# A two-layer encoder trunk on one NeuronCore: the activations' tiles begin 32 bytes later in SBUF, on multiples of 64 bytes, and the weights' tiles keep their place within 64 bytes

## The chip, the cores and the metric

The kernel runs on one core of a Trainium2 chip. The metric is the device time of one execution in microseconds (us); less is better. Before the change it was 1282.45 us, the median of 3 runs (1281.79 to 1290.47). One further execution was recorded by the hardware profiler; it took 1282.87 us.

## The reference, cut to what matters

The input is `x` of 256 positions by 1024 features, all in float32. Two layers of one block follow each other:

```python
for l in range(DEPTH):                                    # 2
    x = x + 0.5 * swiglu(rmsnorm(x, ffn1_norm[l]), ffn1_w_gate[l], ffn1_w_up[l], ffn1_w_down[l])
    proj = rmsnorm(x, mix_norm[l]) @ w_in[l]              # q, k, v, lru x, lru gate, memory q, 3 gates
    ...
    br_attn = window_attention(q, k, v, attn_sinks[l]) @ w_attn_out[l]
    br_lru = rglru_branch(xr, yr, ...) @ w_lru_out[l]
    br_mem = memory_attention(cq, rmsnorm(mem, mem_norm[l]), w_mem_kv[l]) @ w_mem_out[l]
    merged = g[:, :, 0] * br_attn + g[:, :, 1] * br_lru + g[:, :, 2] * br_mem
    x = x + merged @ w_out[l]
    x = x + 0.5 * swiglu(rmsnorm(x, ffn2_norm[l]), ffn2_w_gate[l], ffn2_w_up[l], ffn2_w_down[l])
return rmsnorm(x, final_norm)
```

The feed-forward width is 2816. The weights are some 226 MB in float32, read once, and nearly all of the arithmetic is their products with 256 columns of activations.

## The kernel before, in words

**The weights.** They are packed on the host as 432 slabs of 8 blocks; a block is 128 by 128. `load` (L176 to L180) brings a slab of 512 KB from HBM into one of 5 `st` tiles. `prep` splits it in two parts of type float32r, which TensorE takes in one pass: ScalarE rounds it into `whi` (L194), and VectorE writes the rest, `st - whi`, into `wlo` (L195). There are 5 tiles of each. Loads run up to 5 slabs ahead and splits up to 3 slabs ahead of the block in use.

**The products.** `gemm` goes over the blocks of one 128-row strip of outputs. The activations are split likewise and lie in `Halves` tiles: for each k, 256 columns of the high part and then 256 of the low part. Each block is one matmul of 512 columns (both halves under `whi`, L219) and one of 256 (the high half under `wlo`, L220):

```python
mm(both, hi, X.both(k), start=(k == 0), stop=False)                  # L219
mm(out[:, 0, :], lo, X.hi(k), start=False, stop=(k == n - 1))        # L220
```

The second argument is the stationary operand, which a weight load (`LDWEIGHTS`, PEld in the profile) brings into the array; the third is the moving operand, streamed past it column by column. There are 3,316 such blocks. A few places differ. `mem_kv` makes the values of the memory (tile `mv`, L622 to L624) the other way round: slices of the activations are stationary, and 512 columns of `whi` or `wlo` move. `singles` (L236 to L238, the last 2 strips of the kernel) and the LRU gates take three matmuls of 256 columns to a block. The attention scores and values (`ws`, `ms`, L946) are plain float32, which the array takes in two passes, each of which is a record in the trace.

**The order.** Each engine's instructions stand in the order in which the code is recorded; between the blocks a list of delayed tasks (`at`, `tick`) places the rest of the work, one tick to a slab.

**SBUF.** `pools` opens one pool after another, and each lies behind the one before in every partition. A tile takes a multiple of 32 bytes. The constants come first, then `big` (14 tiles of 8,192 bytes: `x`, all `Halves`, the projections), `h4`, `s2`, `s1`, `sm`, then `stage` (the `st` tiles), and last `hl` (`whi`, `wlo`). The four tiles of the constants take 1,056 + 2,560 + 1,024 + 640 = 5,280 bytes, which is 82 times 64 and 32 more. As they begin on a multiple of 64, every pool behind begins 32 bytes past one, and as nearly all later tiles are multiples of 64 bytes long, so do their tiles: `x` at byte 21,792 of its partition, the first `st` at 166,688, the first `whi` at 187,168. The small `sm` tiles (8 or 16 bytes in 32) alternate.

Of the kernel before, what the change touches and what calls it, by code (L numbers as in the profile page):

```python
# [19 lines left out]
F32 = mybir.dt.float32  # L20
# [74 lines left out]
class Trunk:  # L95
# [17 lines left out]
    def pools(self, ctx):  # L113
        tc = self.tc
        e = ctx.enter_context
        self.pc = e(tc.tile_pool(name="const", bufs=1))
        self.pbig = e(tc.tile_pool(name="big", bufs=14))
        self.ph4 = e(tc.tile_pool(name="h4", bufs=3))
        self.ps2 = e(tc.tile_pool(name="s2", bufs=4))
        self.ps1 = e(tc.tile_pool(name="s1", bufs=3))  # L120
        self.psm = e(tc.tile_pool(name="sm", bufs=2))
        self.pst = e(tc.tile_pool(name="stage", bufs=5))
        self.phl = e(tc.tile_pool(name="hl", bufs=5))
        self.pmm = e(tc.tile_pool(name="mm", bufs=3, space=bass.MemoryType.PSUM))
        self.patt = e(tc.tile_pool(name="att", bufs=2, space=bass.MemoryType.PSUM))
# [931 lines left out]
```

## Time and profile before

| | us | share of the span |
|---|---|---|
| median of 3 runs | 1282.45 | |
| the profiled execution | 1282.87 | |
| its span, first to last instruction | 1281.1 | |
| TensorE matmul (PE) busy | 1265.4 | 99% |
| TensorE weight load (PEld) busy | 1104.4 | 86% |
| VectorE (DVE) busy | 985.7 | 77% |
| ScalarE (ACT) busy | 761.3 | 59% |
| the 16 DMA engines, weights' queue | | 57% |

How to read it: matmuls are pipelined. [...] What a matmul costs the next one is the distance between their starts. PEclk is the granted share of TensorE's clock; at 1.00 it is the upper of the two levels, 2.4 GHz, at which 512 columns at one a cycle are 213.3 ns and 256 are 106.7 ns.

### The profile page before, as it was taken

What the parts mean: (1) busy time and instruction counts of PE and PEld (TensorE: products, weight loads), DVE (VectorE), ACT (ScalarE), POOL (GpSimd) and SP (SyncE); (2) the same over time, 40 slices, a digit from 0 to 9 for tenths busy, and PEclk for the clock granted to TensorE, in tenths of its full rate; (3) what the DMA queues carried; (4) which work ended last, traced back from release to release, by engine and by line L of the source; (5) the groups of instructions that cost most, each with busy time, mean ns of one, the idle gap of its engine ahead of it and who ended that gap; (6) DMA issues with size and microseconds to landing.
All of it is one profiled execution on the core that took longest, in us unless ns stands there. A gap on an engine that the chain in (4) does not pass through costs nothing.

```text
span 1281.1 us, 19099 instructions
## 1 busy us (share of the span) xinstructions
PE 1265.4 (99%) x7318; PEld 1104.4 (86%) x7318; DVE 985.7 (77%) x1406; ACT 761.3 (59%) x1134; POOL 0.3 (0%) x5
## 2 busy tenths in 40 slices
PE   8999999999999999999999999999999999999997
PEld 7888888888888888888888888888888888888886
DVE  7788766888789987677678775669887898876754
ACT  5656544588577565555456564447867675655542
POOL 0000000000000000000000000000000000000000
PEclk9999999999999999999999999999999999999998
DMA  8665665555445566666656665564554465665651
GB/s 288 209 189 167 214 183 179 172 175 166 144 131 187 187 197 189 195 187 202 194 184 208 189 188 195 167 204 156 183 165 132 148 199 180 197 195 185 195 184 48
DMA packets 64748, 232.40 MB, mean 181 GB/s; under 512 B 7313, under 2 KB 7441, under 8 KB 64401
## 3 DMA queue, kind: packets, MB, share of 16 engines
q1 hardware_dynamic: 64224, 230.65, 57.2%
q8 instruction: 58, 0.95, 0.3%
q10 hardware_dynamic: 432, 0.53, 0.1%
q14 instruction: 34, 0.27, 0.1%
HBM read 230.10 MB, written 1.05 MB: 180 GB/s over the span
## 4 chain that ended last, share of the span: by engine, by line
PE 90%; DVE 5%; ACT 3%; issue 1%; DMA 1%; SPq 0%; DVEq 0%; ACTq 0%
PE pd L219 12%; PE pg L219 11%; PE pu L219 11%; PE pd L220 6%; PE pgt L219 6%; PE pu L220 6%; PE pg L220 6%; PE pbr L219 5%; PE pgt L220 3%; DVE wlo L195 2%; PE pyr L219 2%; PE pwo L219 2%; PE pbr L220 2%; PE pxr L219 2%; PE pgu L219 2%; PE pcq L219 1%
## 5 line engine op out<-in xcount | busy, mean ns | idle before, releaser
L195 DVE TENSOR_TENSOR wlo<-st,whi 128x1024 fp32r<-128x1024 f32 (+2 forms) x438 | 524.6, 1206 | 238.1 <-ACT whi L194 238.0
L194 ACT ACTIVATE whi<-st 128x1024 fp32r<-128x1024 f32 (+2 forms) x438 | 443.5, 1045 | 39.5 <-PE pd L219 20.5
L219 PE MATMUL pd<-h,whi 128*128 128x512 f32 x660 | 230.1, 393 | 0.0
L219 PE MATMUL pg<-xs,whi 128*128 128x512 f32 x640 | 225.2, 394 | 0.0
L219 PE MATMUL pu<-xs,whi 128*128 128x512 f32 x640 | 225.1, 393 | 0.0
L220 PE MATMUL pd<-h,wlo 128*128 128x256 f32 x660 | 184.9, 280 | 0.0
L220 PE MATMUL pg<-xs,wlo 128*128 128x256 f32 x640 | 179.3, 280 | 0.8 <-DVE wlo L195 0.8
L220 PE MATMUL pu<-xs,wlo 128*128 128x256 f32 x640 | 179.3, 280 | 0.0
L219 PEld LDWEIGHTS pd<-h,whi 128*128 128x128 f32 x660 | 123.6, 187 | 28.1
L219 PEld LDWEIGHTS pg<-xs,whi 128*128 128x128 f32 x640 | 119.9, 187 | 27.0
L219 PEld LDWEIGHTS pu<-xs,whi 128*128 128x128 f32 x640 | 119.8, 187 | 26.9
L219 PE MATMUL pgt<-xs,whi 128*128 128x512 f32 x384 | 139.2, 405 | 0.0
L220 PEld LDWEIGHTS pd<-h,wlo 128*128 128x128 f32 x660 | 124.7, 189 | 0.0
L220 PEld LDWEIGHTS pg<-xs,wlo 128*128 128x128 f32 x640 | 120.9, 189 | 1.1 <-DVE wlo L195 1.1
L220 PEld LDWEIGHTS pu<-xs,wlo 128*128 128x128 f32 x640 | 121.0, 189 | 0.0
L220 PE MATMUL pgt<-xs,wlo 128*128 128x256 f32 x384 | 107.6, 280 | 0.0
L219 PEld LDWEIGHTS pgt<-xs,whi 128*128 128x128 f32 x384 | 72.1, 188 | 19.5 <-issue 3.0
L258 ACT COPY g<-pg 128x512 f32<-128x512 f32 x40 | 23.5, 586 | 99.7 <-PE pg L220 92.9
L220 PEld LDWEIGHTS pgt<-xs,wlo 128*128 128x128 f32 x384 | 72.5, 189 | 0.2
L270 ACT ACTIVATE h<-u 128x512 fp32r<-128x512 f32 x44 | 27.8, 632 | 46.2 <-DVE u L523 43.9
L320 ACT ACTIVATE xs<-x,pk 128x256 fp32r<-128x256 f32 x40 | 18.7, 503 | 49.2 <-DVE x L559 21.6
L219 PE MATMUL pgu<-xs,whi 128*128 128x512 f32 x128 | 44.7, 394 | 1.2 <-DVE xs L324 1.2
(237 smaller groups left out, 2053.5 us busy)
## 6 DMA issues: line engine op xcount, KB each, us to landing
st<-wpack SPq DMA_DIRECT2D x428, 512.0 KB, 3.8
st<-wpack SPq DMA_DIRECT2D x8, 256.0 KB, 4.9
mem<-memT SPq DMA_DIRECT2D x2, 1024.0 KB, 6.7
x<-xT SPq DMA_DIRECT2D x4, 256.0 KB, 5.0
outT<-xg SPq DMA_DIRECT2D x2, 256.0 KB, 2.6
outT<-xg ACTq DMA_DIRECT2D x2, 256.0 KB, 2.7
cst<-cst SPq DMA_DIRECT2D x1, 320.0 KB, 7.8
pk<-pk SPq DMA_DIRECT2D x1, 128.0 KB, 7.5
```

Source lines behind the costliest of these rows:

```text
L194: nc.scalar.activation(hi[:, c], st[:, c], AF.Copy)
L195: nc.vector.tensor_tensor(lo[:, c], st[:, c], hi[:, c].bitcast(F32), op=ALU.subtract)
L219: mm(both, hi, X.both(k), start=(k == 0), stop=False)
L220: mm(out[:, 0, :], lo, X.hi(k), start=False, stop=(k == n - 1))
L258: self.nc.scalar.copy(dst, ps[:, :, 1, :])
L270: hi = lambda: self.nc.scalar.activation(X.hi(k, n), src, AF.Copy)
L320: self.t.nc.scalar.activation(self.xs.hi(k), x[:, k, :], AF.Copy, scale=self.t.vec(self.v, self.l, k))
```

## The change

Two pools of one tile each are opened that nothing ever uses, each 32 bytes (8 float32) of every partition. `gapx` lies behind the constants and moves all pools behind it by 32 bytes; `gap` lies ahead of `hl` and moves this pool by 32 more.

```diff
         self.pc = e(tc.tile_pool(name="const", bufs=1))
+        e(tc.tile_pool(name="gapx", bufs=1)).tile([128, 8], F32, name="gapx")
         self.pbig = e(tc.tile_pool(name="big", bufs=14))
         self.ph4 = e(tc.tile_pool(name="h4", bufs=3))
         self.ps2 = e(tc.tile_pool(name="s2", bufs=4))
         self.ps1 = e(tc.tile_pool(name="s1", bufs=3))
         self.psm = e(tc.tile_pool(name="sm", bufs=2))
         self.pst = e(tc.tile_pool(name="stage", bufs=5))
+        e(tc.tile_pool(name="gap", bufs=1)).tile([128, 8], F32, name="gap")
         self.phl = e(tc.tile_pool(name="hl", bufs=5))
```

Where the tiles begin, in bytes of a partition, and what is left of that over a multiple of 64:

| tiles | before | over 64 | after | over 64 |
|---|---|---|---|---|
| constants (`pk`, `cst`, `Rm`, `lc`) | 16,512 to 21,152 | 0 or 32 | the same | the same |
| `big` (first: `x`) | 21,792 | 32 | 21,824 | 0 |
| `h4`, `s2`, `s1` (first: `P`) | 136,480 | 32 | 136,512 | 0 |
| `st` | 166,688 | 32 | 166,720 | 0 |
| `whi` | 187,168 | 32 | 187,232 | 32 |
| `wlo` | 207,648 | 32 | 207,712 | 32 |

In the built program every instruction, its place on its engine and its semaphores are the same as before; only addresses differ.

## Rows read from the trace of the kernel before

**Rows 1.** The page: span, busy time by engine, and TensorE's clock in 40 slices.
```profile
span 1281.1 us, 19099 instructions
PE 1265.4 (99%) x7318; PEld 1104.4 (86%) x7318; DVE 985.7 (77%) x1406; ACT 761.3 (59%) x1134; POOL 0.3 (0%) x5
PEclk9999999999999999999999999999999999999998
```
**Rows 2.** The chain of work that ended last, by engine.
```profile
PE 90%; DVE 5%; ACT 3%; issue 1%; DMA 1%; SPq 0%; DVEq 0%; ACTq 0%
```
**Rows 3.** Groups by line, whole span: xcount | busy us, mean ns | idle before.
```profile
L219 PE MATMUL pd<-h,whi 128*128 128x512 f32 x660 | 230.1, 393 | 0.0
L219 PE MATMUL pg<-xs,whi 128*128 128x512 f32 x640 | 225.2, 394 | 0.0
...
L220 PE MATMUL pg<-xs,wlo 128*128 128x256 f32 x640 | 179.3, 280 | 0.8 <-DVE wlo L195 0.8
```
**Rows 4.** TensorE's matmuls in order of time from 500 us: start us, us.
```profile
499.79 0.39 PE L219 MATMUL pu<-xs,whi 128*128 128x512 f32 x1
500.02 0.28 PE L220 MATMUL pu<-xs,wlo 128*128 128x256 f32 x1
...
532.72 0.39 PE L219 MATMUL pu<-xs,whi 128*128 128x512 f32 x1
```
**Rows 5.** The same from 130 us.
```profile
129.62 0.40 PE L219 MATMUL pu<-xs,whi 128*128 128x512 f32 x1
129.86 0.28 PE L220 MATMUL pu<-xs,wlo 128*128 128x256 f32 x1
...
162.84 0.40 PE L219 MATMUL pd<-h,whi 128*128 128x512 f32 x1
```
**Rows 6.** Groups by line, TensorE, 500 to 620 us and then 100 to 200 us.
```profile
L219 PE MATMUL pd<-h,whi 128*128 128x512 f32 x114 | 39.6, 391 | 0.0
L219 PE MATMUL pd<-h,whi 128*128 128x512 f32 x176 | 62.2, 399 | 0.0
```
**Rows 7.** Matmuls in order of time: 512 columns after 512, from 211 us.
```profile
211.30 0.39 PE L622 MATMUL mv<-whi,xs 128*128 128x512 f32 x1
...
214.02 0.39 PE L622 MATMUL mv<-whi,xs 128*128 128x512 f32 x1
```
**Rows 8.** Groups by line, TensorE, 212 to 215, 17.9 to 18.8, 66.0 to 66.5 us.
```profile
L622 PE MATMUL mv<-whi,xs 128*128 128x512 f32 x4 | 1.6, 389 | 0.0
L219 PE MATMUL pg<-xs,whi 128*128 128x512 f32 x1 | 0.4, 389 | 0.0
L220 PE MATMUL pu<-xs,wlo 128*128 128x256 f32 x1 | 0.3, 276 | 0.0
```
**Rows 9.** Weight loads in order of time, 17 to 19 us and at 279.5 us.
```profile
17.67 0.19 PEld L219 LDWEIGHTS pg<-xs,whi 128*128 128x128 f32 x1
18.93 0.19 PEld L220 LDWEIGHTS pg<-xs,wlo 128*128 128x128 f32 x1 [1.07 <-DVE wlo L195]
...
279.53 0.19 PEld L219 LDWEIGHTS pyr<-xs,whi 128*128 128x128 f32 x1
279.63 0.19 PEld L220 LDWEIGHTS pyr<-xs,wlo 128*128 128x128 f32 x1
```
**Rows 10.** The longest pieces of the chain: plain float32 matmuls, start us, us.
```profile
330.08 1.73 PE ms L913 x8
367.72 3.45 PE mv L946 x16
```
**Rows 11.** Matmuls in order of time: 256 columns after 256, 1256 us.
```profile
1256.01 0.28 PE L236 MATMUL pd<-h,whi 128*128 128x256 f32 x1
1256.12 0.28 PE L237 MATMUL pd<-h,whi 128*128 128x256 f32 x1
1256.24 0.28 PE L238 MATMUL pd<-h,wlo 128*128 128x256 f32 x1
1256.37 0.28 PE L236 MATMUL pd<-h,whi 128*128 128x256 f32 x1
```
**Rows 12.** Groups by line and shape: VectorE and ScalarE at 1024 and 512 columns.
```profile
L195 DVE TENSOR_TENSOR wlo<-st,whi 128x1024 fp32r<-128x1024 f32 x428 | 519.2, 1221 | 238.1 <-ACT whi L194 238.0
L508 DVE TENSOR_TENSOR g<-g,R 128x512 f32<-128x512 f32 x44 | 30.4, 692 | 1.5
L194 ACT ACTIVATE whi<-st 128x1024 fp32r<-128x1024 f32 x428 | 438.3, 1056 | 38.9 <-PE pd L219 20.5 <-issue 10.5 <-PE mv L624 4.7
L509 ACT ACTIVATE g<-g 128x512 f32<-128x512 f32 x44 | 27.7, 633 | 27.4 <-DVE g L508 27.1
```
**Rows 13.** Stretches: length, busy us (count) by engine, clock, DMA share, GB/s.
```profile
0.00:30.00 30.00, 25.82 (x143) 22.33 (x144) 22.98 (x51) 19.15 (x30) 0.30 (x5) 1.00 0.86 296
400.00:455.00 55.00, 55.00 (x319) 48.11 (x318) 50.43 (x68) 34.44 (x52) 0.00 (x0) 1.00 0.62 195
455.00:640.00 185.00, 185.00 (x1072) 163.07 (x1071) 133.09 (x172) 101.49 (x130) 0.00 (x0) 1.00 0.62 192
```

## The prediction

> **What bounds the kernel now.** The first view is the page's list of engines [rows 1]: TensorE's matmuls cover 1265.4 of the 1281.1 us, at a granted clock that is full nearly throughout, so at 2.4 GHz. The chain that ended last gives TensorE 90% [rows 2]. VectorE at 77% and ScalarE at 59% keep ahead of it; a group of 640 matmuls waits 0.8 us in all [rows 3]. So the end moves only if TensorE's own pace moves, and the pace has to be read from the distances between starts.
>
> From 499.79 to 532.72 us lie 95 blocks (a matmul of 512 and one of 256 columns each), which is 346.6 ns per block [rows 4]. From 129.62 to 162.84 us lie 94, which is 353.4 ns [rows 5]. At one column a cycle 768 columns would take 320.0 ns. So there are a quick and a slow pace, and both are 27 to 33 ns above the columns' own time. The mean duration of the 512-column matmul tells the pace of a stretch: 391 ns in a quick one, 399 in a slow one [rows 6]. Over the whole span it is 393 and 394 [rows 3], so between a quarter and three eighths of the feed-forward blocks run at the slow pace. With a third, a block takes 348.9 ns, and the 3,316 blocks take 1,157 us.
>
> **Where the loss of a block comes from.** The value product of the memory runs 512 columns after 512: 12 matmuls from 211.30 to 214.02 us, 226.7 ns each, at 389 ns duration [rows 7, 8]. So a record is 162 ns longer than its stream. One matmul of 512 columns ran with no weight load beside it: the next load comes at 18.93 us, 1.15 us after its start (17.78 us), held up by `wlo` [rows 9]. It took 389 ns too [rows 8], a stream of about 227 ns. A lone one of 256 columns took 276 ns, a stream of about 114 [rows 8]. Against 213.3 and 106.7 ns the two lose 13.4 and about 7 ns. The loss without a weight load is thus in proportion to the columns, and close to one cycle of 0.417 ns in 16 columns (32 x 0.417 = 13.3; 16 x 0.417 = 6.7). 16 columns of float32r are 64 bytes of a partition.
>
> The plain float32 matmuls read the same kind of tile, also 32 bytes past a multiple of 64, but take two cycles for each column: 8 records of 256 columns in 1.73 us and 16 in 3.45 us, 216 ns each [rows 10], against 213.3 for 512 cycles. They lose 2.7 ns per record, not 13. So it is the supply of the moving operand that runs short at one float32 a cycle, once in 64 bytes, and at half that rate it keeps up. VectorE and ScalarE show nothing like it: from 512 to 1024 columns VectorE needs 1221 - 692 = 529 ns more and ScalarE 1056 - 633 = 423 [rows 12], steady steps of 1.03 and 0.83 ns, slower than TensorE's 0.417.
>
> **The change part by part.** *The two gaps* add no instruction, no transfer and no wait; the built programs differ in addresses alone. Their direct cost is 0. *The `st` tiles* move too, which touches the DMAs that write them and the first operand of each split; both run ahead of TensorE, and a gain there stays hidden. *The weights' tiles* keep their place within 64 bytes, so a weight load by itself keeps its time: two in a row start 0.10 us apart at 279.53 us [rows 9]. *The moving operand of nearly all matmuls* now begins on a multiple of 64. Before, each run of 16 columns counted from the operand's start lay across two 64-byte lines; now it lies in one. No matmul in this trace has a start of the other kind at one float32 a cycle, so the price is bounded from both sides.
>
> Bound of no gain: the cycle is lost at each crossing of a line, and 512 columns make 32 of them (now 31): 0 us. Bound of full gain: the loss goes, and what the two-cycle matmuls lose stays, 2.7 ns [rows 10]. Then 512 columns take 216.0 ns and 256 take 109.4, a block 325.4, and the sum is 3,316 x (348.9 - 325.4) = 78 us. Between them: the 256-column matmul may be held by the load of the next weights rather than by its stream. Three such matmuls in a row start at 1256.01, 1256.12, 1256.24 and 1256.37 us, 120 ns each [rows 11], more than the stream of 114, and a block at the quick pace leaves 346.6 - 230 = 117 ns for it [rows 4]. With 216.0 + 116.7 = 332.7 a block gains 16.2 ns, the sum 54 us. If also the slow pace with its 6.8 ns stayed everywhere, 339.5 remain and 31 us are gained. I take 54 us, since the rows of 256 after 256 say that this matmul waits for more than its columns. The value product and `singles` gain nothing: in the one the weights move, and the other stands at 120.
>
> *What takes some of it back.* In the first 30 us TensorE waits for data at 296 GB/s (25.82 of 30 us busy) [rows 13]; some 60 blocks gain nothing, 1 us. VectorE is busiest between 400 and 455 us, 50.43 of 55 [rows 13]; at a pace 4.6% quicker this is 96%, so it still fits. The weights come at 192 GB/s in a steady stretch [rows 13] and would come at 201, below the 296 of the start. So 53 us remain: 1282.9 - 53 = 1230. The profiled execution stands 0.4 us above the median, which I neglect.
>
> [...]
>
> **The rivals.**
> *Nothing changes (1282 us).* The cycle in 64 bytes may belong to the crossing itself, or to float32r at full rate, wherever the operand begins. For it: every start in the trace is alike, so nothing in it shows a dependence, and the distances are regular to a nanosecond over 33 us. Against it: nothing, but a read path that falls short by one cycle in 17 for every operand would be odd. The slow and quick paces may be dealt out anew, as they follow interruptions: all quick is 3,316 x 2.3 = 8 us less (1275), all slow 3,316 x 4.5 = 15 us more (1297).
> *A smaller gain.* Only the slow pace goes, or only the 512-column stream gains a part: 1251 to 1268 us. I count this with the first case as "faster".
> *Slower.* Moving and stationary operand began at the same place within 64 bytes, and now begin half a line apart. The weight load beside a 512-column matmul is free at best now (389 ns with and without [rows 8]). If the two reads come to meet, every block pays for it. The place is each block; the price is bounded by the slow pace everywhere, 1297 us, and by the longest distances within it, about 0.24 us for a 512-column matmul and 0.12 for a 256 (129.62 to 129.86 us is the former [rows 5]), 360 ns a block, 37 us, 1320. It decides as soon as the loss per block exceeds 4 ns. [...]
>
> **How the numbers follow.** I give the gain (1204 to 1268 us, likeliest 1230) 0.43, no change (1275 to 1297) 0.37, the loss (1297 to 1320) 0.20. The likeliest is the gain, and its own range is 1204 to 1252. Both signs hold much of the chance, so the range of 8 in 10 reaches from 1208 (some 0.04 lie below) to 1301 (some 0.16 above). About 1%, 13 us, is what a measurement of this kernel can tell from no change. Faster by more than that: 0.43; within: 0.37; slower: 0.20.
>
> **What would show it.** If the step is right, a quick stretch shows blocks of 325 to 333 ns, the 512-column matmul at about 378 ns instead of 391, the value product unchanged at 389 (its moving operand stays 32 past a line), and the plain float32 matmuls unchanged at 216. If the rival of no change holds, 391 and 346.6 stand as they were. If the reads meet, the 512-column matmul grows above 399 ns and the 256-column one with it, and the value product, whose two operands now differ as well, grows too. My forecast is wrong if the lost cycle stays with operands that begin on a line, or if the 256-column matmul takes up what the 512 gives.

## The result, and the profile after

The changed kernel takes **1293.18 us** (1291.48 to 1294.36), against 1282.6 for the kernel before in the same rounds: a ratio of 1.008, 95% interval 1.0063 to 1.0096. Forecast were 1230. The time moved by less than 1%, and to the other side.

The page of the changed kernel, its span, engines and clock, answers to [rows 1]:

```profile
span 1290.9 us, 19099 instructions
PE 1276.4 (99%) x7318; PEld 1107.9 (86%) x7318; DVE 985.9 (76%) x1406; ACT 762.5 (59%) x1134; POOL 0.3 (0%) x5
PEclk9999999999999999999999999999999999999998
```

TensorE alone has grown, its matmuls by 11.0 us of busy time at the same count of instructions and the same clock; VectorE and ScalarE stand where they were. The page's groups by line (two lines of code are added, so L221 is L219 of before, and L222 is L220) answer to [rows 3]:

```profile
L221 PE MATMUL pd<-h,whi 128*128 128x512 f32 x660 | 233.4, 397 | 0.0
L221 PE MATMUL pg<-xs,whi 128*128 128x512 f32 x640 | 227.8, 397 | 0.0
L222 PE MATMUL pg<-xs,wlo 128*128 128x256 f32 x640 | 180.0, 281 | 0.0
```

The 512-column matmul did not fall from 391 to the 378 ns of a right forecast. Its mean went from 393 and 394 to 397, to the side of the slow pace. The matmuls in order of time from 500 us, the stretch of [rows 4] (start us, us):

```profile
499.94 0.40 PE L221 MATMUL pu<-xs,whi 128*128 128x512 f32 x1
500.18 0.28 PE L222 MATMUL pu<-xs,wlo 128*128 128x256 f32 x1
500.30 0.39 PE L221 MATMUL pu<-xs,whi 128*128 128x512 f32 x1
500.53 0.28 PE L222 MATMUL pu<-xs,wlo 128*128 128x256 f32 x1
500.64 0.40 PE L221 MATMUL pu<-xs,whi 128*128 128x512 f32 x1
...
532.80 0.39 PE L221 MATMUL pu<-xs,whi 128*128 128x512 f32 x1
```

From 499.94 to 532.80 us lie 93 blocks, 353.3 ns each, where the kernel before ran at 346.6 [rows 4]. So no new pace came, but the slow one where the quick one was. In detail it is another slow pace: here two blocks repeat (0.36 and 0.35 us), while the slow stretch of before [rows 5] repeats after three. Over the two traces, with a block called quick where the mean distance of the seven around it is under 350 ns (distances over 390 ns, which hold a wait, left out), the kernel before has 2,144 quick ones of 3,263 in a row and the changed one 548; the mean of either kind is nearly the same in both, 346.7 and 353.3. (2,144 - 548) x 6.6 ns = 10.5 us, which is the whole difference of the medians (10.6).

The stretches answer to [rows 13] (length, busy us and count by engine, clock, DMA share, GB/s): in the same 185 us TensorE starts 1,053 matmuls where it started 1,072.

```profile
400.00:455.00 55.00, 55.00 (x314) 47.75 (x313) 49.89 (x67) 33.45 (x51) 0.00 (x0) 1.00 0.59 193
455.00:640.00 185.00, 185.00 (x1053) 160.85 (x1052) 131.28 (x170) 101.12 (x130) 0.00 (x0) 1.00 0.60 186
```

And the value product, 512 columns after 512, in order of time [rows 7]:

```profile
211.18 0.39 PE L626 MATMUL mv<-whi,xs 128*128 128x512 f32 x1
211.41 0.40 PE L624 MATMUL mv<-whi,xs 128*128 128x512 f32 x1
...
213.28 0.39 PE L626 MATMUL mv<-whi,xs 128*128 128x512 f32 x1
```

Nine distances in 2.10 us are 233.3 ns, against 226.7 before. This is the sign that the prediction named for two reads that meet, though its moving operand (the weights) keeps its place within 64 bytes.

**The theories.** A: the step of the prediction, an operand that begins on a multiple of 64 loses no cycle (fallen with the result, unless the weights' own place hid the gain). B: the pace hangs on the place of the weights against that of the activations, modulo 64 bytes. C: the same, but modulo a longer period (the change moves the weights from a distance of 0 to one of 32 modulo 512). D: only the instant at which a stretch begins deals out the pace. I first thought of B; C came out of the bursts and the padded tiles below.

### The profile page after: what moved, and what is told of

Read it like the earlier page. It is cut to its first block, busy times and chain, and to the rows that moved or that the text cites. A ratio compares the mean times of both kernels' runs of the same rounds, so it can differ in the third digit from the quotient of the medians.

```text
span 1290.9 us, 19099 instructions
## 1 busy us (share of the span) xinstructions
PE 1276.4 (99%) x7318; PEld 1107.9 (86%) x7318; DVE 985.9 (76%) x1406; ACT 762.5 (59%) x1134; POOL 0.3 (0%) x5
## 4 chain that ended last, share of the span: by engine, by line
PE 92%; DVE 4%; ACT 2%; issue 1%; DMA 1%; SPq 0%; DVEq 0%; ACTq 0%
PE pd L221 12%; PE pg L221 11%; PE pu L221 11%; PE pgt L221 7%; PE pd L222 6%; PE pu L222 6%; PE pg L222 6%; PE pbr L221 5%; PE pgt L222 3%; PE pyr L221 2%; PE pbr L222 2%; PE pwo L221 2%; DVE wlo L197 2%; PE pxr L221 2%; PE pgu L221 2%; PE pwo L222 1%
## 5 line engine op out<-in xcount | busy, mean ns | idle before, releaser
L221 PE MATMUL pd<-h,whi 128*128 128x512 f32 x660 | 233.4, 397 | 0.0
L221 PE MATMUL pu<-xs,whi 128*128 128x512 f32 x640 | 228.0, 397 | 0.0
L221 PE MATMUL pg<-xs,whi 128*128 128x512 f32 x640 | 227.8, 397 | 0.0
L222 PE MATMUL pd<-h,wlo 128*128 128x256 f32 x660 | 185.8, 282 | 0.0
L222 PE MATMUL pu<-xs,wlo 128*128 128x256 f32 x640 | 180.0, 281 | 0.0
L222 PE MATMUL pg<-xs,wlo 128*128 128x256 f32 x640 | 180.0, 281 | 0.0
L221 PEld LDWEIGHTS pd<-h,whi 128*128 128x128 f32 x660 | 123.9, 188 | 30.7
L221 PEld LDWEIGHTS pu<-xs,whi 128*128 128x128 f32 x640 | 120.2, 188 | 29.2
L221 PEld LDWEIGHTS pg<-xs,whi 128*128 128x128 f32 x640 | 120.1, 188 | 29.1
L221 PE MATMUL pgt<-xs,whi 128*128 128x512 f32 x384 | 139.0, 403 | 0.0
L222 PEld LDWEIGHTS pd<-h,wlo 128*128 128x128 f32 x660 | 124.4, 188 | 0.0
L222 PEld LDWEIGHTS pu<-xs,wlo 128*128 128x128 f32 x640 | 120.6, 189 | 0.0
L222 PEld LDWEIGHTS pg<-xs,wlo 128*128 128x128 f32 x640 | 120.6, 188 | 0.0
L222 PE MATMUL pgt<-xs,wlo 128*128 128x256 f32 x384 | 107.9, 281 | 0.0
L221 PEld LDWEIGHTS pgt<-xs,whi 128*128 128x128 f32 x384 | 72.1, 188 | 19.3 <-issue 2.3
L222 PEld LDWEIGHTS pgt<-xs,wlo 128*128 128x128 f32 x384 | 72.4, 189 | 0.2
L221 PE MATMUL pgu<-xs,whi 128*128 128x512 f32 x128 | 45.3, 396 | 1.0 <-ACT whi L196 1.0
```

## The experiments

### The places within 64 bytes, one by one

`act0_w0` opens `gapx` alone, so that activations and weights both begin on multiples of 64. `act32_w0` opens `gap` alone: the activations stay, and the weights move by 32. `all_64on` moves everything by 64 bytes, which keeps every residue modulo 64.

```diff
# act0_w0                                  # all_64on: [128, 16]
+ e(tc.tile_pool(name="gapx", bufs=1)).tile([128, 8], F32, name="gapx")
# act32_w0, ahead of hl
+ e(tc.tile_pool(name="gap", bufs=1)).tile([128, 8], F32, name="gap")
```

> Only gapx, so every tile behind the constants begins on a multiple of 64: moving and stationary operand lie alike again, as in the kernel before. Theory of the distance (the pace is worse where the two operands begin half of 64 bytes apart): blocks in layer 1's feed-forward parts at 346.6 ns, time 1275 to 1286 us. Theory of the moving operand (its start on a multiple of 64 is what costs): 353.5 ns per block and 1291 to 1295 us, as after the change. Theory of the deal (no address matters; each waiting point deals the quick or the slow pace anew): anywhere from 1275 to 1297 us.

> Only gap, so the activations stay 32 bytes past a multiple of 64 and the weights' tiles begin on one: half of 64 bytes apart, the other way round than after the change. Theory of the distance: 353.5 ns per block nearly throughout, 1291 to 1295 us. Theory of the moving operand: as before, 1281 to 1286 us, quick blocks of 346.6 ns in layer 1. Theory of the deal: anywhere from 1275 to 1297 us.

> gapx of 64 bytes alone: all tiles behind the constants move by 64, so nothing changes modulo 64 against the kernel before. Theories of the distance and of the moving operand: 1281 to 1286 us and the stretches of quick and slow blocks where they were. If residues modulo 128 or more matter, or if the paces are dealt anew by chance, the stretches change: anywhere from 1275 to 1297 us.

Measured: `act0_w0` 1291.65 us, ratio 1.008 (1.0059 to 1.0102); `act32_w0` 1294.32, 1.0103 (1.008 to 1.0126); `all_64on` 1287.75 (1282.8 to 1292.6), 1.0048 (1.0013 to 1.0082). The 512-column group `pd` in the pages of `act0_w0`, `act32_w0` and `all_64on`, in this order:

```profile
L220 PE MATMUL pd<-h,whi 128*128 128x512 f32 x660 | 233.4, 399 | 0.0
```
```profile
L220 PE MATMUL pd<-h,whi 128*128 128x512 f32 x660 | 232.2, 396 | 0.0
```
```profile
L220 PE MATMUL pd<-h,whi 128*128 128x512 f32 x660 | 233.4, 399 | 0.0
```

A falls: with both operands on multiples of 64 the matmul takes 399 ns, the slow pace of before, and no stretch comes near the 325 to 333 ns of a right forecast. Of the three theories in the expectations, that of the distance had allowed at most 1286 us to `act0_w0` and `all_64on`, and that of the moving operand at most 1286 to `act32_w0` and `all_64on`; only the deal, with its wide range of 1275 to 1297, holds for all three. The slow pattern follows the distance of weights and activations: three blocks repeat in `act0_w0` and `all_64on` (distance 0, as before), two in `act32_w0` (distance 32, as after). But at distance 0 the share of quick blocks is 769 and 579 of 3,263 here against 2,144 before. So the distance gives the kinds of pace, and something else chooses between them.

### Bursts of matmuls alone

`bench_offsets` and `bench_deal` run bursts one behind another with next to no other work beside them, with starts in two tiles shifted by 0 (a), 16 (b), 32 (c) and 48 bytes (d), first the moving operand's letter, then the weights'. `bench_deal` begins each burst after a matmul of another length, repeats each pair 8 times, and has two more kinds: every second column of a tile (512 columns over 4,096 bytes), and bfloat16.

```python
mm(ps[:, 0:lead], st[:, s:s + 128], mv[:, m:m + lead])          # the instant
mm(ps[:, 0:c], st[:, a:a + 128], mv[:, b:b + step * c:step])    # c = 512, 256, 512, ...
```

> Nothing of the trunk is computed (the output is the input): bursts of matmuls alone on two tiles that begin alike modulo 512, read at start offsets of 0, 16, 32 and 48 bytes (letters a, b, c, d: first the moving operand's, then the stationary's), as blocks of 512 and 256 columns (blk), 512 alone (wide) and 256 alone (thin); e to h are 64, 96, 128 and 256 bytes, i and j 4 and 8 bytes. My step of the lost cycle in 64 bytes with a start off a line: blka* streams 512 columns in 216 ns, blkb* to blkd* in 227 to 230; it has already failed in the kernel, so I expect 227 to 230 in all. Theory of the distance: mean durations depend on the difference of the two letters alone, lowest (391 ns for 512) where the letters are equal, highest (397 to 399) where they differ by 32 bytes. Theory of the moving operand: rows of one first letter read alike. Theory of the deal: means of 391 to 399 without any order by letters, and differing between repeats of one pair.

> Nothing of the trunk is computed (the output is the input). Bursts of 16 blocks (512 and 256 columns) for each of the 16 pairs of start offsets 0, 16, 32, 48 bytes (a to d, moving first), each pair in 8 bursts that a matmul of 64 to 176 columns opens, so that they begin at other instants. Theory of the deal: most pairs show the quick 346.6 ns in some of their bursts and 353.3 or another pace in others; the offsets only shift the odds. Theory of the distance: all 8 bursts of a pair run alike. Side tests of the lost cycle: a lone matmul with no weight load beside it (lonew, lonet) takes 389 and 276 ns at every start if the loss does not depend on the start, 378 where it does; bfloat16 operands (bfwide) take 216 ns if the loss comes from 4 bytes a column at full rate; every second column of the tile (skip), 32 bytes of data in each 64, takes about 240 ns if the loss is one cycle per 64 bytes passed, 227 if it is one per 16 columns.

Measured, in ns per block: aa is 346.7 in some bursts and 353.3 in others, cc too (four and four), and ac, the distance of the changed kernel, likewise (four and four). In ac the quick four are those behind the shorter opening matmuls (64 to 112 columns), in cc those behind the longer (128 to 176), so what runs ahead of a burst seems to bear on its pace, though aa shows no such order. ad, ba, ca and cd are at 346.7 in all eight, bc at 353.3 in all eight, bd at 343.3 in seven. As ac and bd both have the weights 32 bytes on, the distance alone doesn't fix the kinds of pace when starts move by 16 bytes. With the moving operand at 0 and the weights 64, 96, 128 and 256 bytes on, `bench_offsets` shows 353.3, 346.7, 351.1 and 353.3; modulo 64 the 64 and the 128 should read alike, and 351.1 is no pace of aa. 512 after 512 take 226.7 ns for aa and cc, 233.3 for ac and ca: the value product before and after. A moving start 4 bytes on (ia) is the slowest, 360.0 in both bursts.

The lost cycle is settled by the other kinds. In order of time in `bench_deal`, records of one kind in a row (start us, us from the first start to the last end, count):

```profile
820.19 7.88 PE L52 MATMUL skipa<-mv,st 128*128 128x512 f32 x17
```
```profile
837.54 4.26 PE L66 MATMUL bfwide<-hm,hs 128*128 128x512 bf16 x19
```
```profile
844.01 2.67 PE L66 MATMUL bfthin<-hm,hs 128*128 128x256 bf16 x23
```

With the record 162 ns longer than its stream, every second column takes (7.88 - 0.62) / 16 = 0.454 us, twice 226.7, for the same 512 columns over twice the bytes (and neither of the 240 and 227 ns that I had expected). bfloat16, half the bytes, takes (4.26 - 0.38) / 18 = 0.2156 and (2.67 - 0.27) / 22 = 0.1091 us. There 256 columns more are 106.5 ns, 2.40 columns a ns at a granted clock of 9 tenths or more in the page; this is the 2.4 GHz by which cycles are counted here, one bfloat16 column in each. By estimate from these times the moving operand comes in at 64 bytes of a partition in 17 such cycles: 4,096 bytes are 64 x 17 = 1,088 cycles or 453.3 ns, 2,048 are 544 or 226.7 ns, and 1,024 in bfloat16 need 272, fewer than their 512 columns. A start on a multiple of 64 doesn't give the cycle back: aa and cc take the same 226.7, and every second column takes 453 from either start. The floor of a block by this estimate is (32 + 16) x 17 = 816 cycles, **340.0 ns**.

The matmuls that ran alone between waits missed the 389 and 276 ns expected of them, but they say more. In `bench_deal`, 512 and 256 columns alone, and the clock where most of them ran (the figure before the DMA share):

```profile
L58 PE MATMUL lonewc<-lo,st 128*128 128x512 f32 x4 | 3.2, 793 | 1.9 <-ACT lo L59 1.9
L58 PE MATMUL lonetc<-lo,st 128*128 128x256 f32 x4 | 2.3, 580 | 2.7 <-ACT lo L59 2.7
```
```profile
854.00:865.00 11.00, 5.81 (x9) 2.29 (x8) 0.00 (x0) 4.43 (x9) 0.00 (x0) 0.50 0.00 0
```

At a granted clock of 0.50, 256 columns more take 793 - 580 = 213 ns, twice the 106.5 of bfloat16 at full clock, so with nothing lost; the few alone at full clock (497 and 384 ns at 849.45 and 850.64 us) differ by 113, half of 226.7. This fits a limit of supply in time, by estimate 226.7 / 32 = 7.1 ns for 64 bytes, where TensorE at half its clock takes 213 / 16 = 13.3 ns over them; that it is such a limit is my reading of the times.

### The weights at 16 and 48 bytes

> gapx, and the split weights read 16 bytes into their tiles: moving operand on a multiple of 64, stationary 16 bytes past one (pair ab of the bench, quick in 8 bursts of 8). Theory of the odds (the pair of offsets sets which paces can lock, the instant of the start picks among them): all blocks quick, 346.6 ns in every stage, time 1274 to 1277 us and little spread. Theory of a deal by instants alone, whatever the offsets: a mixture as in the other versions, 1280 to 1295 us.

> gapx, and the split weights read 48 bytes into their tiles: pair ad of the bench, also quick in 8 of 8, though 512 columns after 512 took 233.3 ns there. Theory of the odds: blocks of 346.6 ns in every stage, 1274 to 1278 us. Deal by instants alone: 1280 to 1295 us.

> Activations left 32 bytes past a multiple of 64 as in the kernel before, the split weights read 16 bytes into their tiles, 48 past one: pair cd, quick in 8 of 8. Theory of the odds: blocks of 346.6 ns in every stage, 1274 to 1277 us. Deal by instants alone: 1280 to 1295 us. If this and act0_w16 come out alike, it is the distance of 16 bytes that counts and not where the moving operand starts.

```diff
+ OFF = 4                                                        # 12
- hi = self.phl.tile([128, HB * 128], F32R, tag="hi", name=f"whi_{s}")
+ hi = self.phl.tile([128, HB * 128 + 16], F32R, tag="hi", name=f"whi_{s}")[:, OFF:OFF + HB * 128]
```

Measured: 1285.44, 1285.88 and 1285.69 us, each with its runs within 0.6 to 1.4 us of one another, ratios 1.0024 to 1.0027; the 1274 to 1278 expected of a quick pair are missed in all three. The pace does not lock any more: 349.6 or 349.7 ns per block on average in the three traces, and 348 to 352 in their stages, the group `pd` at 394 or 395 ns. I had taken 16 and 48 bytes modulo 64 for the variable. The 64 bytes of padding in each tile change more: the tiles are 4,160 bytes apart, so the distance moves by 64 bytes from one tile to the next of the five. In the trace of `act0_w16` some 21 quick blocks come every 14 us, which is 40 blocks or five tiles of 8. Under B all tiles are alike; that the pace follows the tile speaks for C.

### The period

`bench_512` runs bursts of nine blocks for sixteen starts of the 512-column matmuls' weights (first letter) by sixteen of the 256-column matmuls' (second), a to p for 0 to 480 bytes.

> Bursts of nine blocks (512 after 256 columns) alone, for sixteen starts of the 512-column matmuls' weights by sixteen starts of the 256-column matmuls' weights, in steps of 32 bytes through 512 bytes, the activations always at the same start; three bursts of each pair. The trunk is left out (the output is a copy of the input). If the pace hangs on starts modulo 512 bytes, the pairs fall into paces between about 343 and 360 ns per block that repeat over the three bursts and that don't repeat when a start moves by 64 bytes; some pairs are always at 346.7 or below. If only residues modulo 64 matter, the 256 pairs fall into four groups, (0 or 32) by (0 or 32), each with one pace or one mixture. If the instant alone deals the pace, every pair shows quick and slow bursts, about half and half.

Four of the pairs, in order of time, third bursts: bb (the changed kernel's distances), pp, fd and gi.

```profile
1735.75 0.40 PE L43 MATMUL blkbb<-mv,hi 128*128 128x512 f32 x1
1735.99 0.28 PE L44 MATMUL blkbb<-mv,lo 128*128 128x256 f32 x1
1736.11 0.39 PE L43 MATMUL blkbb<-mv,hi 128*128 128x512 f32 x1
...
1737.87 0.40 PE L43 MATMUL blkbb<-mv,hi 128*128 128x512 f32 x1
```
```profile
2511.52 0.39 PE L43 MATMUL blkpp<-mv,hi 128*128 128x512 f32 x1
...
2513.25 0.39 PE L43 MATMUL blkpp<-mv,hi 128*128 128x512 f32 x1
```
```profile
1951.01 0.40 PE L43 MATMUL blkfd<-mv,hi 128*128 128x512 f32 x1
...
1953.13 0.40 PE L43 MATMUL blkfd<-mv,hi 128*128 128x512 f32 x1
```
```profile
2019.80 0.39 PE L43 MATMUL blkgi<-mv,hi 128*128 128x512 f32 x1
2020.02 0.28 PE L44 MATMUL blkgi<-mv,lo 128*128 128x256 f32 x1
2020.14 0.39 PE L43 MATMUL blkgi<-mv,hi 128*128 128x512 f32 x1
...
2021.50 0.39 PE L43 MATMUL blkgi<-mv,hi 128*128 128x512 f32 x1
```

bb takes 2.12 us for 6 blocks, 353 ns, with the two-block pattern of the changed kernel; pp 1.73 for 5, 346; fd 2.12 for 6, 353; gi 1.70 for 5, 340.0, the floor. Over the last six distances of a burst, a start of the 512-column matmuls' weights 256 bytes on gives a pace less than 1 ns away in 383 of 383 comparisons; one 32 bytes on, in 156 of 719; 64 on, in 118 of 671; 128 on, in 99 of 575. For the 256-column matmuls' weights it is 329 of 383 at 256 bytes, 139 of 671 at 64. So the period of the weights' start is 256 bytes, not 64 (and not 512, which I had written). Without the program's first burst, which takes 640 ns a block, paces go from 340 to 355 ns, and 127 of the 256 pairs have bursts over 1 ns apart.

### Three places chosen from the table, in the kernel

```diff
# w_480on: all weights 480 bytes on (pp)
+ e(tc.tile_pool(name="gap", bufs=1)).tile([128, 120], F32, name="gap")
# w_hi192_lo256 (gi): 192 bytes ahead of whi, 64 more ahead of wlo; w_hi160_lo96 (fd): 160 and 448
+ e(tc.tile_pool(name="gap", bufs=1)).tile([128, 48], F32, name="gap")
  self.phl = e(tc.tile_pool(name="hl", bufs=5))
+ e(tc.tile_pool(name="gap2", bufs=1)).tile([128, 16], F32, name="gap2")
+ self.pll = e(tc.tile_pool(name="ll", bufs=5))
- lo = self.phl.tile(...)
+ lo = self.pll.tile(...)
```

> The activations stay where the kernel before has them; all weights move by 480 bytes, so that the residues modulo 64 bytes are those of act32_w0 (activations 32 past, weights on multiples of 64) and the distance is minus 32 modulo 512 in place of plus 32. By distance modulo 512: the pair that was at 346.7 ns in eleven bursts of eleven, so nearly all blocks at 346.6 and 1274 to 1277 us. By residues modulo 64: as act32_w0, 1291 to 1295 us. By the instants alone: anywhere from 1280 to 1295 us, with quick and slow stages.

> The activations stay; the 512-column matmuls' weights start 160 bytes on and the 256-column matmuls' weights 608 bytes on (96 modulo 512), residues modulo 64 bytes as in w_480on and act32_w0 (activations 32, weights 0). By distance modulo 256 or 512: a pair that ran at 353 ns per block in all three bursts, so nearly all blocks at 353 ns, 1294 to 1298 us. By residues modulo 64: one time for act32_w0, w_480on and this kernel, which w_480on's 1276.5 us already speaks against. By the instants alone: anywhere from 1275 to 1297 us, a mixture of stages at 346.7 and 353.

> The activations stay; the 512-column matmuls' weights start 192 bytes on and the 256-column matmuls' weights 256 bytes on, all residues modulo 64 bytes as in the kernel before (32, 32, 32). By distance modulo 256 or 512: the one pair that ran at 340.0 ns per block in all three of its bursts, so nearly all of the 3,316 blocks at 340 to 341 ns in place of 348.9 on average, 26 to 30 us less, 1252 to 1257 us. By residues modulo 64: the kernel before, 1279 to 1290 us. By the instants alone: anywhere from 1275 to 1297 us, never below 1274.

Measured: `w_480on` **1276.54** us (1276.14 to 1277.3), ratio 0.9953 (0.9933 to 0.9973); `w_hi160_lo96` **1296.24** (1295.79 to 1296.59), 1.0097 (1.0067 to 1.0127); `w_hi192_lo256` **1270.79** (1259.0 to 1273.92), 0.9889 (0.9844 to 0.9934). The stretch of 185 us in the three, in this order, to be read beside 1,072 before [rows 13] and 1,053 after:

```profile
455.00:640.00 185.00, 185.00 (x1072) 164.09 (x1071) 130.11 (x168) 100.20 (x128) 0.00 (x0) 1.00 0.61 191
```
```profile
455.00:640.00 185.00, 185.00 (x1052) 161.00 (x1051) 131.25 (x170) 100.46 (x129) 0.00 (x0) 1.00 0.60 187
```
```profile
455.00:640.00 185.00, 185.00 (x1092) 163.67 (x1091) 132.56 (x170) 103.94 (x134) 0.00 (x0) 1.00 0.62 191
```

`w_480on` has 3,253 quick blocks of 3,263, at 346.7 ns, and `w_hi160_lo96` has 43, the rest at 353.3. `act32_w0`, `w_480on` and `w_hi160_lo96` have one residue modulo 64 (activations 32, weights 0), yet `w_480on` lies 18 and 20 us below the other two, while `w_hi192_lo256` has the residues of before and runs a pace that no trace of it shows: B falls. D falls as the whole answer: two places hold one pace each through all stages of their traces, and the runs of each lie within 1.2 us of one another, where the kernel before, unedited, spreads from 1278.9 to 1294.3 over the rounds of these experiments. `w_hi192_lo256` reached my 1252 to 1257 in none of its runs, because its pair has two paces in the kernel. In order of time, from 500 us and from 99:

```profile
499.76 0.39 PE L222 MATMUL pg<-xs,whi 128*128 128x512 f32 x1
...
532.74 0.39 PE L222 MATMUL pg<-xs,whi 128*128 128x512 f32 x1
```
```profile
98.86 0.40 PE L222 MATMUL pu<-xs,whi 128*128 128x512 f32 x1
...
132.81 0.40 PE L222 MATMUL pu<-xs,whi 128*128 128x512 f32 x1
```

97 blocks take 32.98 us, 340.0 ns each, and 97 take 33.95, 350.0 each. In the whole trace 2,174 run about 340.4 and 1,084 at 350.0. Beside 340, the table had shown 350 for the pair ga, which differs from gi by 256 bytes in the second place, the place whose period held in 329 of 383: a burst of nine blocks had not met it.

### What chooses between two paces of one place

Three kernels keep their addresses and get 24 matmuls of 96 columns more, each ahead of the first block of a group of weights.

```diff
+ if k == 0 and blocks[k][:2] not in self.seen:
+     self.seen.add(blocks[k][:2])
+     mm(both[:, 0:96], hi, X.both(k)[:, 0:96], start=True, stop=True)
```

> The kernel before with all starts as they are, and 24 matmuls of 96 columns more, one ahead of the first block of each group of weights (24 by about 43 ns, 1 us of added work). If the instant at which a stretch begins deals between the two paces that distance 0 allows, stages change their pace: the quick blocks are no longer 2,144 in the same places, and the time lies anywhere from 1276 to 1298 us. If the starts alone set the pace, the quick blocks stay where they are and the time is 1282 to 1284 us, or 1 us above the kernel before in the same rounds.

> w_480on with the same 24 matmuls. If its distance allows one pace alone (quick in eleven bursts of eleven and in 3,253 of 3,263 blocks), the instants change nothing: 1276 to 1279 us. If w_480on was a lucky deal, stages fall to 353 ns and the time is 1280 to 1295 us.

> w_hi192_lo256, which showed two paces (340.4 ns in 2,174 blocks, 350.0 in 1,084), with the same 24 matmuls. If the instant deals between these two, other stages run at 340 and 350, and the time lies between 1254 (all 340) and 1286 us (all 350), elsewhere than 1271 us by more than 2 us; no block runs at 346.7 or 353. If the starts alone decide, the same stages stay slow and the time is 1271 to 1273 us.

Measured: 1283.35 us (ratio 1.0013, 1.0003 to 1.0023), 1279.35 (0.9986, 0.9976 to 0.9995) and **1263.28** (1262.23 to 1264.03; 0.986, 0.9843 to 0.9876). In `b_lead96` the total is what the starts alone would give, but the stages are not. The group `pd` from 75 to 215 us, which takes 399 ns in the kernel before [rows 6], is here (L223 for L219):

```profile
L223 PE MATMUL pd<-h,whi 128*128 128x512 f32 x176 | 61.1, 391 | 0.0
```

204 blocks from 135 us turned quick, 61 at 434 and as many at 1064 turned slow, and the sum came to 2,177 quick ones by chance. `w_480on_lead96` stays quick in 3,224 of 3,242; its time, just outside the 1276 to 1279 expected, is 2.8 us above `w_480on`, of which the added matmuls are 1 and 1.8 are not accounted for. In `w_192_256_lead96` the last stage changed from 350 to 340.4 ns (2,817 of 3,242 blocks at 340.4, though 90 from 218 us went the other way), and with it the median is the best of all, 19 us below the kernel before. So at one place stages change their pace, and where the place allows one pace they don't. That it was the added matmuls that changed them is not shown: each kernel has one trace, and the executions of `w_hi192_lo256` alone, with nothing changed, spread from 1259.0 to 1273.9 us, around the 1263.28. That the instant at which a stretch begins chooses among the paces of a place is the likely reading, argued from this and from the opening matmuls of ac and cc.

## Why the prediction was wrong, point by point

- **TensorE bounds, and only its pace moves the end: right.** Every profiled time above follows from the mean distance of blocks, to within 4 us. `w_480on`: (348.9 - 346.8) x 3,263 = 7 us expected of the traces, 6 measured.
- **One cycle is lost in 64 bytes, in proportion to columns, for want of supply: right, as far as the times tell.** Half the bytes lose it not (bfloat16, 215.6 ns for 512 columns and 109.1 for 256), twice the bytes take twice 226.7 ns (454), and at a granted clock of 0.50 it is gone (213 ns for 256 columns more). No row of before gives the 2.4 GHz behind the 213.3 and 106.7 ns; the 106.5 ns of 256 bfloat16 columns in `bench_deal` bear it out.
- **The cycle comes from a start 32 past a multiple of 64 bytes, so an aligned start gives it back: wrong, and this is the step that failed.** The rows of before only showed that the loss goes with bytes, and all starts in them were alike, as the text itself said for its rival of no change. It chose the start as cause because a path that is short by one cycle in 17 "would be odd". It is so: `act0_w0` has aligned starts and gains nothing (1291.65 us, 399 ns for 512 columns), and `w_hi192_lo256` reaches the floor of 340.0 ns with its moving operand 32 past a multiple of 64. The 54 us (and 78, and 31) all hang on this step.
- **The 256-column matmul is held by the next weights, not by its stream (120 ns): left as it was.** Bursts of 256 after 256 in `bench_offsets` run at 116.7 to 120 ns by place, against 113.3, half of 226.7.
- **The slow pace was treated as a term that the change may or may not take along (31 us case), or as dealt anew (rival of no change).** This was the whole effect. The rival's own bounds, all quick 1275 and all slow 1297, are met by `w_480on` (1276.5) and `w_hi160_lo96` (1296.2), and the changed kernel lies at 1293.2 between them.
- **The rival "slower" had the right sign and the right witness.** It said that moving and stationary starts, which had been in one place, would lie apart, that the slow pace would spread, and that the value product would grow; all three are so. Its unit was wrong (half of 64 bytes): `w_480on` lies half of 64 bytes apart too, and is quicker than before. Its 0.20 was my estimate. The runs show that the place of one read bears on the pace: moving the weights alone, at the same work, gives 340.0 (`w_hi192_lo256`) to 353.3 ns a block (`w_hi160_lo96`).
- **The unknown instant.** `act0_w0` and `all_64on` keep the distance of before and still stand 9 and 5 us above its 1282.45, so of the 10.6 us of the change a part may be the new distance (its two-block pattern, the value product) and a part what the stretches drew. The two are not separated: at distance 32 some bursts are quick too (four of eight). How a pace comes out of place and instant, and whether it is the two reads of TensorE that meet in something with a period of 256 bytes, is argued from the table, not shown. The kernel before reaches 1294.3 us in a single execution with no edit, so such a time is open to its own distance too. Also not shown is why a move of everything by 32 or 64 bytes deals otherwise than before.

## What to carry over

Where TensorE is the bound, read its pace from the distances between starts, and look for two paces in the same code (346.7 and 353.3 ns a block here): if they are there, the places of the two operands against each other, modulo 256 bytes here, are worth a table from a short burst program before any of them is moved. Before a loss is given a cause that the trace holds constant, such as a start that all rows share, a burst that varies it alone costs less than the change does. A wide spread over executions of one program, 1278.9 to 1294.3 us here, may be a sign of the same thing. A version whose place showed one pace alone (`w_480on`, 1276.1 to 1277.3 us) is the steady choice; one with a better second pace (`w_hi192_lo256`, 1259.0 to 1273.9 us) is faster and can change from one execution to the next.

## What had not been expected of the hardware

- float32r takes 226.7 ns for 512 columns and 454 with every second column, against 215.6 in bfloat16; by estimate that is 64 bytes of a partition in 7.1 ns. At a granted clock of 0.50 it loses nothing (213 ns for 256 columns more, twice the 106.5 of bfloat16).
- A block of 512 and 256 columns locks into one of several paces, in the kernel 340.0, 346.7, 350.0 or 353.3 ns for hundreds of blocks, in bursts 343.3 too; the places of the weights modulo 256 bytes have much to say in which are open (256 bytes on, the pace is less than 1 ns away in 383 of 383 comparisons for the 512-column matmuls' weights and in 329 of 383 for the others').
- With the same addresses and instructions, one program (`w_hi192_lo256`) took 1259.0 to 1273.9 us, and another (`w_480on`) 1276.1 to 1277.3.
